# Sums over a head's 64 channels: one fp32 product, or two fp32r products on data split into high and low parts

## The chip, the cores and the metric

The kernel runs on one core of a Trainium2 chip. The metric is the device time of one execution in microseconds (us). Matrix products run on TensorE (PE in the profile), elementwise work on VectorE (DVE), ScalarE (ACT) and GpSimd (POOL), and transfers are started by SyncE (SP).

## The reference, cut to what matters

One layer of a streaming encoder is computed for 1024 prompt frames and 64 sample frames. Each frame is normed, projected to 3336 columns, and split between an RWKV-7 group (8 heads of 64 channels, with a recurrent state) and a forgetting-attention group (8 heads of 64 channels). The two are joined, projected, and followed by a SwiGLU feed-forward part. Five places need, for each head and frame, a sum or a mean over the head's 64 channels:

```
kk = kk / jnp.maximum(jnp.linalg.norm(kk, axis=-1, keepdims=True), 1e-12)
bonus = (jnp.sum(rh * kh * r_k, axis=-1, keepdims=True) * vh).reshape(b, t, RWKV_WIDTH)
mu = jnp.mean(y, axis=-1, keepdims=True)
var = jnp.mean(jnp.square(y - mu), axis=-1, keepdims=True)
q = _rms_norm(_heads(q, FOX_HEADS), fox_q_g)      # and the same for the keys
```

All of it is fp32.

## The kernel before, in words

**Layout.** Channels lie on the 128 partitions and frames along the free axis, so that one tile holds two heads (a pair is called j, 0 to 3). The frames are cut into two halves: half 0 has 512 frames, half 1 has 512 and the 64 sample frames, 576 in all. A half's `chunks` (L46) are the pieces that one product covers: one of 512 columns, or two of 288.

**Large products** are made from fp32r operands, each split into a high part (a rounding copy on ACT) and a low part (the difference, on DVE), as three products: high by high, high by low, low by high (`mm3`, L318). The projections write the PSUM tile `pmm` this way.

**Sums over a head** are made by `bsum` (L398): a product with a 128x128 matrix of ones in two 64x64 blocks (`bones`), or of 1/64 (`bmean`). Both matrices and the data are plain fp32, and there is one product for each chunk. The PSUM tile is `pbs`. There are 48 calls, 24 for each half: per head pair two in `rwkv_a` (on `sq` and on `zr`, which is a tile called `z` in the profile), two in `rwkv_n` (on `y` and on its squares, `gsq`), and two in `fox_norm` (on `fsq`, for queries and keys).

**The stages of an RWKV head pair.** `Z` makes three projections, `D` the decays, `A` (`rwkv_a`) the sums, the products `pA` and a small triangular inverse that goes through DRAM, `B` (`rwkv_b`) first completes the inverse with small products (`pg`, `pw`, `pu`, `pgt`) and then runs the scan: 8 or 9 steps, each of the products `pR`, `pSA`, `pS` and two `pY`, with copies on DVE and ACT between them, each step waiting for the one before it. `N` (`rwkv_n`) normalises `y`. The stages `Q`, `K` project attention's queries and keys and `q`, `k` norm them; `V` makes values, `L` the forget biases, `O` writes rows of ones. The two strings in L35 are the order in which the program writes these stages for the two halves. In half 0 it reads `... A0 D1 Z1 L Q0 B0 V0 N0 A1 ...`, so `A1` is written behind `N0`. In half 1 it has `A2 k0 D3 Q1 q0 N0 B1`.

**What sets the order of the work.** A scheduler takes the program's instructions and puts each engine's in an order of its own: what is ready goes first, and among what is ready what was written first. Tiles come from pools; a pool has a number of slots for each tag, and a tile that finds no free slot holds its first writer back. Among the tags are `ms` (one slot in the kernel before), `sa`, `fx` (4 slots: two pairs of `fraw` and `fsq`), `rk` and `kb` (2 slots each), and for PSUM `ra`, `rb`, `fx`, `ch`, `mm`. `bsum` in `A` writes to `ra`, in `N` to `rb`, in `q` and `k` to `fx`. What fills PE between the steps of a scan is mostly projections.

**Attention** follows: eight heads of half 0 (`attend`), whose products of queries and keys are `psc`, with a product that adds the causal mask (`cmask`, L943); `ppt` are transposes and `pav` the products with the values. `att_pools` (L863) makes the mask in a slot of `ms` (`cm`, L871 to 876). The last `N3` of half 1 is written after the order strings are through (L1478) and ahead of attention. Then attention of half 1, the output projection, and the feed-forward part follow, none of which uses `bsum`.

Of the kernel before, what the change touches and what calls it, by code (L numbers as in the profile page):

```python
# [7 lines left out]
F32 = mybir.dt.float32  # L8
F32R = mybir.dt.float32r
BF16 = mybir.dt.bfloat16  # L10
AF = mybir.ActivationFunctionType
ALU = mybir.AluOpType
# [4 lines left out]
P = 128  # L17
# [3 lines left out]
SS = 64  # L21
# [43 lines left out]
class K:  # L65
# [47 lines left out]
    def consts2(self):  # L113
        nc, A = self.nc, self.A
        c, f = self.cpool, self.fper
        self.bones = f.tile([P, P], F32, name="bones")
        self.bmean = f.tile([P, P], F32, name="bmean")
        for t, v in ((self.bones, 1.0), (self.bmean, 1.0 / 64)):
            nc.gpsimd.memset(t, 0.0)
            nc.gpsimd.memset(t[0:64, 0:64], v)  # L120
            nc.gpsimd.memset(t[64:128, 64:128], v)
        self.tri = f.tile([P, P], F32, name="tri")
        nc.gpsimd.memset(self.tri, 1.0)
        nc.gpsimd.affine_select(out=self.tri, in_=self.tri, compare_op=ALU.is_ge, fill=0.0, base=0,
# [271 lines left out]
            evac(ps[:, 0:n], off, n)  # L396

    def bsum(self, hf, w, x, evac, tag):  # L398
        nc = self.nc
        for off, n in hf.chunks:  # L400
            ps = self.ps([P, 512], tag=tag, name="pbs")
            nc.tensor.matmul(ps[:, 0:n], w, x[:, off:off + n], start=True, stop=True)  # L402
            evac(ps[:, 0:n], off, n)

    def split_lora(self, hf, z):
# [280 lines left out]
    def logf(self, hf):  # L686

        nc, O = self.nc, self.O
# [6 lines left out]
        for off, n in hf.chunks:  # L695
            ps = self.ps([P, 512], tag="mm", name="pfl")
# [8 lines left out]
        for i in range(nt):  # L705
            m = P if i < 4 else SS
# [4 lines left out]
        w = self.fpool.tile([P, 5, 8], F32, tag="lfw", name="lfw")  # L711
# [33 lines left out]
            nc.gpsimd.tensor_copy(keep, acc)  # L745
            self.lacc = keep

        q4 = self.fpool.tile([P, 7, 4, 8], F32, tag="lq", name="lq")
        hi = self.fpool.tile([P, 7, 2, 8], F32R, tag="lh", name="lh")
        for i, _, _, _, _ in order:  # L750
            nc.vector.tensor_copy(hi[:, i, 0], pl[:, i])
# [5 lines left out]
        for g in (order[0:4], order[4:]):  # L757
# [11 lines left out]
            w = sum(m for _, _, _, m, _ in g)  # L769
# [67 lines left out]
    def by_tokens(self, hf, j, src):  # L837
        nc = self.nc
        pt = self.ps([P, 4, P], tag="fx", name="pkv")
        for i in range(4):  # L840
            nc.tensor.transpose(pt[:, i], src[:, i * P:(i + 1) * P], self.ident)
        dst, ds_ = self.slot([P, 4, P], name="tok", tag="fx"), None
        nc.scalar.copy(dst, pt)
        nc.sync.dma_start(self.O["fox_v"][j, :, 4 * hf.i:4 * hf.i + 4], dst)
        if hf.smp:
            pt = self.ps([SS, P], tag="fx", name="pkvs")
            nc.tensor.transpose(pt, src[:, 512:576], self.ident)
            ds_ = self.fpool.tile([SS, P], F32, tag="toks", name="toks")
            nc.scalar.copy(ds_, pt)
            nc.sync.dma_start(self.O["fox_v"][j, 0:SS, 8], ds_)  # L850
        return dst, ds_
# [518 lines left out]
    def run(self):  # L1370
        tc, nc, A, O = self.tc, self.nc, self.A, self.O
        halves = [Half(0), Half(1)]
        with ExitStack() as top:
            E = lambda es, name, bufs=1, **k: es.enter_context(tc.tile_pool(name=name, bufs=bufs, **k))
# [20 lines left out]
            mid = top.enter_context(ExitStack())  # L1395
            self.cmid = E(mid, "cmid")
            self.consts()
            self.spool = MultiPool({"mrow": E(mid, "smrow", 2), "mred": E(mid, "smred", 2)})
            self.spool.pools.update({"ms": E(mid, "sms", 1)})
            hst = top.enter_context(ExitStack())  # L1400
            hp = E(hst, "hpool", side="right")
            self.hhi = hp.tile([P, KT, 576], F32R, name="hhi")
# [2 lines left out]
            with ExitStack() as es:  # L1405
# [3 lines left out]
                hf = halves[0]  # L1409
# [4 lines left out]
                raw, w = [], []  # L1414
# [26 lines left out]
            E = lambda es, name, bufs=1, **k: E0(es, name, bufs, **{"reuse_waits": "tile", **k})  # L1441
# [8 lines left out]
            FP = lambda p, tags: MultiPool({t: E(fxs, p + t, b, side="right") for t, b in tags})  # L1450
            RP = lambda p, tags: MultiPool({t: E(rws, p + t, b) for t, b in tags})
            self.rpool.pools.update(RP("r", (("pp", 1), ("pb", 2), ("mb", 1), ("wb", 1), ("tb", 1), ("xl", 1))).pools)
            self.spool.pools.update(RP("s", (("sa", 4),)).pools)
            self.fpool = FP("f", (("toks", 1), ("lfu", 1), ("lfe", 1), ("lfw", 1), ("lacc", 2), ("lq", 1), ("lh", 1)))
            self.spool.pools.update(FP("s", (("fx", 4),)).pools)
            self.ops = {}

# [11 lines left out]
            for hf in halves:  # L1469
                if hf.i:  # L1470
                    for k in range(KT):
                        x = self.zpool.tile([P, 576], F32, tag="z", name="xk")
# [81 lines left out]
            acc, raw, w, ada = None, [], {}, []  # L1554
# [208 lines left out]
```

## Time and profile before

| | |
|---|---|
| time, median of 3 runs | 1698.58 us (1694.36 to 1699.02) |
| profiled execution, span from first to last instruction | 1691.4 us |
| median less span | 7.2 us |
| PE busy | 1642.2 us, 97% |
| DVE busy | 1122.1 us, 66% |
| ACT busy | 725.6 us, 43% |
| mean granted PE clock | 0.992 |
| `bsum` products, first and last | 68.9 us, 722.6 us |

The profile is of one execution, and gives no time of its own beside the span; what lies around the span is taken as the 7.2 us between it and the median. [...] One fp32 product is two MATMUL rows in the trace and one row in the order.

### The profile page before, as it was taken

What the parts mean: (1) busy time and instruction counts of PE and PEld (TensorE: products, weight loads), DVE (VectorE), ACT (ScalarE), POOL (GpSimd) and SP (SyncE); (2) the same over time, 40 slices, a digit from 0 to 9 for tenths busy, and PEclk for the clock granted to TensorE, in tenths of its full rate; (3) what the DMA queues carried; (4) which work ended last, traced back from release to release, by engine and by line L of the source; (5) the groups of instructions that cost most, each with busy time, mean ns of one, the idle gap of its engine ahead of it and who ended that gap; (6) DMA issues with size and microseconds to landing.
All of it is one profiled execution on the core that took longest, in us unless ns stands there. A gap on an engine that the chain in (4) does not pass through costs nothing.

```text
span 1691.4 us, 33224 instructions
## 1 busy us (share of the span) xinstructions
PE 1642.2 (97%) x12891; PEld 1438.5 (85%) x12891; DVE 1122.1 (66%) x2561; ACT 725.6 (43%) x1524; POOL 184.7 (11%) x412
## 2 busy tenths in 40 slices
PE   6999999999999999989999999999999999999999
PEld 3776776788888888667889899999999999999998
DVE  6776676757867655886887985555555556545545
ACT  4535364653545345775776633333333333111210
POOL 2102230222121212201220000000000000000000
PEclk9999999999999999998999999999999999999999
DMA  8544447541233344466564532222222215423313
GB/s 310 163 129 132 141 136 201 175 124 33 72 85 85 81 136 115 144 203 177 156 194 153 178 121 78 77 77 77 78 77 77 77 65 178 146 87 97 97 38 125
DMA packets 133580, 207.08 MB, mean 122 GB/s; under 512 B 62126, under 2 KB 70350, under 8 KB 133422
## 3 DMA queue, kind: packets, MB, share of 16 engines
q1 hardware_dynamic: 133422, 204.95, 39.6%
q8 instruction: 102, 1.67, 0.4%
q14 instruction: 56, 0.46, 0.1%
HBM read 157.65 MB, written 47.25 MB: 121 GB/s over the span
## 4 chain that ended last, share of the span: by engine, by line
PE 85%; ACT 5%; DVE 5%; DMA 4%; issue 2%; SPq 0%; ACTq 0%; DVEq 0%
PE pd L1302 15%; PE pfe L1187 8%; PE pfc L1187 7%; PE pfa L1187 7%; PE pmm L321 5%; PE pmm L322 5%; PE pmm L323 5%; PE pfb L1187 4%; PE pbs L402 2%; PE pav L989 2%; PE ppt L967 2%; PE pA L491 2%; PE po L321 2%; PE po L322 2%; PE po L323 2%
## 5 line engine op out<-in xcount | busy, mean ns | idle before, releaser
L321 PE MATMUL pmm<-hhi,whi 128*128 128x288 f32 (+1 forms) x624 | 218.2, 350 | 2.4 <-ACT pb L344 1.4
L322 PE MATMUL pmm<-hlo,whi 128*128 128x288 f32 (+1 forms) x624 | 216.4, 347 | 0.7 <-DVE hlo L299 0.7
L323 PE MATMUL pmm<-hhi,wlo 128*128 128x288 f32 (+1 forms) x624 | 214.7, 344 | 0.6 <-DVE wlo L243 0.6
L239 ACT CAST whi<-wraw 128x1024 fp32r<-128x1024 f32 (+2 forms) x116 | 99.2, 855 | 210.0 <-PE pd L1302 163.6
L1302 PE MATMUL pd<-al,whi 128*128 128x512 f32 (+1 forms) x528 | 172.4, 326 | 0.0
L1302 PE MATMUL pd<-ah,whi 128*128 128x512 f32 (+1 forms) x528 | 172.2, 326 | 0.0
L1302 PE MATMUL pd<-ah,wlo 128*128 128x512 f32 (+1 forms) x528 | 172.2, 326 | 0.0
L1306 DVE SCALAR_TENSOR_TENSOR x1t<-pd,mod,x1t 128x512 f32<-128x512 f32 x192 | 91.2, 498 | 106.6 <-PE pd L1302 105.9
L321 PEld LDWEIGHTS pmm<-hhi,whi 128*128 128x128 f32 x624 | 118.4, 190 | 13.9 <-ACT pb L344 2.0
L322 PEld LDWEIGHTS pmm<-hlo,whi 128*128 128x128 f32 x624 | 118.2, 189 | 10.9 <-DVE hlo L299 1.4
L323 PEld LDWEIGHTS pmm<-hhi,wlo 128*128 128x128 f32 x624 | 118.1, 189 | 10.7 <-issue 1.7
L243 DVE TENSOR_TENSOR wlo<-wraw,whi 128x1024 fp32r<-128x1024 f32 (+2 forms) x108 | 104.2, 964 | 19.5 <-ACT whi L239 18.7
L1302 PEld LDWEIGHTS pd<-ah,whi 128*128 128x128 f32 x528 | 99.1, 188 | 7.1
L1302 PEld LDWEIGHTS pd<-ah,wlo 128*128 128x128 f32 x528 | 99.1, 188 | 7.1
L1302 PEld LDWEIGHTS pd<-al,whi 128*128 128x128 f32 x528 | 99.1, 188 | 6.9
L1187 PE MATMUL pfc<-hh,hS 128*128 128x256 f32 (+1 forms) x352 | 101.8, 289 | 1.1 <-ACT hh L1089 1.1
L1187 PE MATMUL pfa<-hh,whi 128*128 128x256 f32 (+1 forms) x352 | 102.1, 290 | 0.0
L1187 PE MATMUL pfc<-hh,lS 128*128 128x256 f32 (+1 forms) x352 | 101.8, 289 | 0.0
L1187 PE MATMUL pfa<-hl,whi 128*128 128x256 f32 (+1 forms) x352 | 101.6, 289 | 0.0
L1187 PE MATMUL pfa<-hh,wlo 128*128 128x256 f32 (+1 forms) x352 | 101.5, 289 | 0.0
L1187 PE MATMUL pfc<-hl,hS 128*128 128x256 f32 (+1 forms) x352 | 100.7, 286 | 0.0
L631 POOL TENSOR_SCALAR sd<-sv,pc 64x64 f32<-64x64 f32 x136 | 77.0, 566 | 181.3 <-DVE sv L644 157.7
(368 smaller groups left out, 4380.7 us busy)
## 6 DMA issues: line engine op xcount, KB each, us to landing
wraw<-in_w_in_dram SPq DMA_DIRECT2D x52, 512.0 KB
wada<-in_w_ada_dram SPq DMA_DIRECT2D x48, 512.0 KB
as<-actscr SPq DMA_DIRECT2D x22, 544.0 KB
wraw<-in_w_gate_dram SPq DMA_DIRECT2D x22, 512.0 KB
wraw<-in_w_up_dram SPq DMA_DIRECT2D x22, 512.0 KB
wraw<-in_w_down_dram SPq DMA_DIRECT2D x40, 256.0 KB
wraw<-in_w_out_dram SPq DMA_DIRECT2D x16, 512.0 KB
actscr<-sg SPq DMA_DIRECT2D x22, 288.0 KB
```

What stands on the lines that cost most here:

```text
L239: nc.scalar.copy(hi, src)
L243: eng.tensor_tensor(lo, src, hi.bitcast(F32), op=ALU.subtract)
L321: nc.tensor.matmul(ps[0:M, 0:n], whi[:, k, 0:M], xhi[:, k, off:off + n], start=(k == 0), stop=False)
L322: nc.tensor.matmul(ps[0:M, 0:n], whi[:, k, 0:M], xlo[:, k, off:off + n], start=False, stop=False)
L323: nc.tensor.matmul(ps[0:M, 0:n], wlo[:, k, 0:M], xhi[:, k, off:off + n], start=False, stop=(k == kt - 1))
L402: nc.tensor.matmul(ps[:, 0:n], w, x[:, off:off + n], start=True, stop=True)
L491: nc.tensor.matmul(pa[h][:, i], kb[hp, c + i], rk[hp, c + i], start=True, stop=True)
L631: nc.gpsimd.tensor_scalar(sd[hsl[h]], sv[hsl[h], c, h], pc[hsl[h], c], None, op0=ALU.mult)
L967: nc.tensor.transpose(pt[0:rows, b - b0, t * P:t * P + qn], p[0:qn, pc:pc + rows], self.ident[0:qn, 0:qn])
L1187: nc.tensor.matmul(ps, l[:, k], r[:, s, k], start=(first and k == 0 and y == 0), stop=(k == 3 and y == 2), skip_group_check=True)
L1302: nc.tensor.matmul(ps[:, 0:n], w[:, i], x[:, t:t + n], start=(i == 0 and y == 0), stop=(i == len(fs) - 1 and y == 2))
L1306: nc.vector.scalar_tensor_tensor(dst, ps[:, so - off:so - off + l], self.mod[:, 40 + o, b:b + 1], dst, op0=ALU.mult, op1=ALU.add)
```

## The change

`bsum` splits its data into a high part (copy to fp32r on ACT) and a low part (difference on DVE), both in a new tile `bhl`, and makes two fp32r products, ones by high and ones by low, that add up in PSUM. `bones` and `bmean` become fp32r. The pieces are 256 columns in half 0 and 288 in half 1, so half 0 has two for each call, and its PSUM tiles and evacuations are of 256 columns. `bhl` is a tile of `ms`, which gets three slots. To make room, two small tiles (`lq`, `toks`) move from pools of their own to slots of `ms` and `mrow`.

```diff
     def consts2(self):
-        self.bones = f.tile([P, P], F32, name="bones")
-        self.bmean = f.tile([P, P], F32, name="bmean")
...
+        self.bones = f.tile([P, P], F32R, name="bones")
+        self.bmean = f.tile([P, P], F32R, name="bmean")
+        blk = self.slot([P, P], name="blk")
...
+        nc.vector.tensor_copy(self.bones, blk)
+        nc.vector.tensor_scalar(self.bmean, blk, 1.0 / 64, None, op0=ALU.mult)
...
     def bsum(self, hf, w, x, evac, tag):
-        for off, n in hf.chunks:
+        m = 288 if hf.smp else 256
+        for off, n in ((o, m) for o in range(0, hf.n, m)):
+            hl = self.slot([P, 2, 288], F32R, name="bhl")[:, :, 0:n]
+            nc.scalar.copy(hl[:, 0], x[:, off:off + n])
+            nc.vector.tensor_tensor(hl[:, 1], x[:, off:off + n], hl[:, 0].bitcast(F32), op=ALU.subtract)
             ps = self.ps([P, 512], tag=tag, name="pbs")
-            nc.tensor.matmul(ps[:, 0:n], w, x[:, off:off + n], start=True, stop=True)
+            for i in range(2):
+                nc.tensor.matmul(ps[:, 0:n], w, hl[:, i], start=(i == 0), stop=(i == 1))
             evac(ps[:, 0:n], off, n)
...
-        q4 = self.fpool.tile([P, 7, 4, 8], F32, tag="lq", name="lq")
+        q4 = self.slot([P, 7, 4, 8], name="lq")
...
-            ds_ = self.fpool.tile([SS, P], F32, tag="toks", name="toks")
+            ds_ = self.slot([P, P], name="toks", tag="mrow")[0:SS]
...
-            self.spool.pools.update({"ms": E(mid, "sms", 1)})
+            self.spool.pools.update({"ms": E(mid, "sms", 3)})
```

The change also moves work on every engine. Throughout the changed kernel the casts into `bhl` stand in the order in which the program makes the tiles. Three places follow; a number behind a name tells tiles of one name apart, and line numbers of the changed kernel are larger by 8 behind `bsum`.

ACT, first half, before: `sq_1151` is the tile of `A1`, and L460 and L461 work on its sums. These rows stand 76 rows ahead of the first row of `N0` on this engine (the squares `gsq_1791`).

```order
L703 COPY fl_1263<-pfl_1267 128x512
L194 COPY mrow_1360<-pada_1351 128x128
L460 ACTIVATE sq_1151<-sq_1151 128x512
L718 ACTIVATE lfe_1291<-lfu_1290 128x32
L461 ACTIVATE sq_1151<-sq_1151 128x512
L719 ACTIVATE lfe_1291<-lfe_1291 128x32
```

ACT, first half, changed: `y_1585` and `gsq_1818` are tiles of `N0`, `sq_1167` is the tile of `A1`.

```order
L406 CAST bhl_1811<-y_1585 128x256
L241 CAST whi_2799<-wraw_2797 128x1024
L196 COPY mrow_2740<-pada_2731 128x128
L672 ACTIVATE gsq_1818<-y_1585 128x512
L406 CAST bhl_1820<-gsq_1818 128x256
L406 CAST bhl_1827<-gsq_1818 128x256
L406 CAST bhl_1843<-sq_1167 128x256
L674 ACTIVATE gsq_1818<-pbs_1823,eps_g_156 128x256
L406 CAST bhl_1850<-sq_1167 128x256
```

The sums of `A1` moved from well ahead of `N0` to behind both sums of `N0`, and with them what needs them: the `pA` products of `A1` and its inverse.

PE, half 1, the middle of the scan of pair 0, before: one step from its `pR` on, with projections (`pmm`) between its products.

```order
L624 MATMUL pR<-sv,At 128x128
L635 MATMUL pY<-rk,sv 128x128
L322 MATMUL pmm<-hlo,whi 128x288
L323 MATMUL pmm<-hhi,wlo 128x288
L321 MATMUL pmm<-hhi,whi 128x288
L637 MATMUL pSA<-R,inv_692 128x64
L322 MATMUL pmm<-hlo,whi 128x288
L323 MATMUL pmm<-hhi,wlo 128x288
L321 MATMUL pmm<-hhi,whi 128x288
L322 MATMUL pmm<-hlo,whi 128x288
```

PE, the same scan, changed: two of its last five steps, all of which look like this.

```order
L632 MATMUL pR<-sv,At 128x128
L643 MATMUL pY<-rk,sv 128x128
L645 MATMUL pSA<-R,inv_686 128x64
L648 MATMUL pS<-sv,kb 128x128
L653 MATMUL pY<-At,sv 128x128
L632 MATMUL pR<-sv,At 128x128
L643 MATMUL pY<-rk,sv 128x128
L645 MATMUL pSA<-R,inv_686 128x64
L648 MATMUL pS<-sv,kb 128x128
L653 MATMUL pY<-At,sv 128x128
```

No projection stands between their products any more. The scan of pair 2 of this half has six such steps at its end, and those of pair 2 in half 0 and pair 3 in half 1 have some too. After the small products that follow this scan, PE has 20 `bsum` products in a row.

PE, the end of half 1, before: attention's first rows, the mask among them. They stand ahead of the first `pR` of the last scan (pair 3).

```order
L937 MATMUL psc<-k1x_8027,qsx_8025 128x256
L939 MATMUL psc<-k2x_8028,q2x_8026 128x256
L943 LDWEIGHTS identb
L943 MATMUL psc<-cmask,identb 128x128
L550 MATMUL pu_8122<-inv_693,g_8059 32x32 x18
L841 MATMUL pkv<-ident,fv 128x128 x2
```

PE, the end of half 1, changed: the last step of the last scan, and the first rows with the mask.

```order
L632 MATMUL pR<-sv,At 128x128
L645 MATMUL pSA<-R,inv_687 128x64
L643 MATMUL pY<-rk,sv 128x128
L648 MATMUL pS<-sv,kb 128x128
L653 MATMUL pY<-At,sv 128x128
L410 MATMUL pbs<-bhl,bmean 128x288 x6
L951 LDWEIGHTS identb
L951 MATMUL psc<-cmask,identb 128x128
```

The mask, and with it all of attention but four `psc` products, moved from ahead of the last scan to behind it and behind six of the eight products of `N3`. On POOL the instruction that fills `cm` moved from an early place in half 0 to behind the last scan's rows (`sd`).

## The prediction on record

> **What bounds the kernel now.** I read first the page's busy line, which names PE.
>
> ```profile
> PE 1642.2 (97%) x12891; PEld 1438.5 (85%) x12891; DVE 1122.1 (66%) x2561; ACT 725.6 (43%) x1524; POOL 184.7 (11%) x412
> ```
>
> A busy share over the whole span can hide a stage with another limit, so the timeline was next, for marks. A scan begins with a `pR`; these are the first `pR` of the first scan, the second, the fourth, the fifth and the last, with the first product of the last `N` behind them.
>
> ```profile
> 148.76 0.46 PE L624 MATMUL pR<-sv,At 128*128 128x128 f32 x2
> 211.50 0.46 PE L624 MATMUL pR<-sv,At 128*128 128x128 f32 x2
> 378.30 0.46 PE L624 MATMUL pR<-sv,At 128*128 128x128 f32 x2
> 468.73 0.46 PE L624 MATMUL pR<-sv,At 128*128 128x128 f32 x2
> 678.36 0.46 PE L624 MATMUL pR<-sv,At 128*128 128x128 f32 x2
> 717.43 0.70 PE L402 MATMUL pbs<-y,bmean 128*128 128x288 f32 x2
> ```
>
> Between these marks the windows view gives PE alone: the stretch, its length, PE's busy time, the granted clock.
>
> ```profile
> 0.00:148.80 148.80, 131.32 (x1142) 0.98 0.58 194
> 148.80:211.50 62.70, 61.35 (x544) 1.00 0.46 131
> 211.50:378.30 166.80, 161.75 (x1408) 0.99 0.55 161
> 378.30:468.70 90.40, 88.40 (x830) 1.00 0.20 49
> 468.70:678.40 209.70, 204.99 (x1947) 0.99 0.39 103
> 678.40:717.40 39.00, 35.19 (x229) 1.00 0.50 149
> 717.40:945.00 227.60, 218.71 (x1330) 0.97 0.60 175
> ```
>
> In every stretch but the first, where loads come in, PE is busy for 90% or more. Two things run side by side: a chain (sums, inverse, scan, norm, pair after pair), which is a matter of waits, and projections, which fill PE while the chain waits. So PE's work sets the time only as long as there is something to fill with. The rest of the span, behind 945 us, has no `bsum`, and I leave it as it is.
>
> **What the change takes from PE.** These rows give the distance between ends: a 512-column fp32 product behind the product before it, a 288-column one likewise, and neighbours of 256 and 288 columns among the fp32r products of the feed-forward part.
>
> ```profile
> 68.53 0.50 PE L321 MATMUL pmm<-hhi,whi 128*128 128x512 f32 x1
> 68.87 1.02 PE L402 MATMUL pbs<-sq,bones 128*128 128x512 f32 x2
> 551.73 0.29 PE L323 MATMUL pmm<-hhi,wlo 128*128 128x288 f32 x1
> 551.86 0.65 PE L402 MATMUL pbs<-sq,bones 128*128 128x288 f32 x2
> 1100.77 0.29 PE L1187 MATMUL pfb<-hl,hS 128*128 128x288 f32 x1
> 1100.90 0.30 PE L1187 MATMUL pfb<-hh,lS 128*128 128x288 f32 x1
> 1110.15 0.28 PE L1187 MATMUL pfa<-hh,whi 128*128 128x256 f32 x1
> 1110.27 0.28 PE L1187 MATMUL pfa<-hl,whi 128*128 128x256 f32 x1
> ```
>
> The view of L402 counts the fp32 products by shape, two MATMULs each; the `z`, `y` and `gsq` groups have the counts of `sq`.
>
> ```profile
> L402 PE MATMUL pbs<-fsq,bones x48: 404/432/697, 154.5 to 653.8; 128*128 128x288 f32 x32, 128*128 128x512 f32 x16
> L402 PE MATMUL pbs<-sq,bones x24: 403/406/697, 68.9 to 552.1; 128*128 128x288 f32 x16, 128*128 128x512 f32 x8
> ```
>
> 512 columns: 69.89 less 69.03 is 0.86 us. 288 columns: 552.51 less 552.02 is 0.49. The new ones: 0.12 for 256, 0.13 for 288. A call in half 0 goes from 0.86 to 4 x 0.12 = 0.48, and 24 of them save 9.1 us. A piece in half 1 goes from 0.49 to 0.26, and 48 save 11.0. In all 20 us leave PE, 1.2% of the time. If PE's work were all, that would be the result.
>
> **What it adds.** 96 casts and 96 subtracts. The nearest rows are those of attention's `pth` and `ptl`, of 256 columns.
>
> ```profile
> 718.50 0.37 ACT L980 CAST pth<-ppt 128x256 fp32r<-128x256 f32 x1 [0.49 <-PE ppt L967]
> 720.58 0.40 DVE L981 TENSOR_TENSOR ptl<-ppt,pth 128x256 fp32r<-128x256 f32 x1
> ```
>
> 96 x 0.37 is 36 us on ACT and 96 x 0.40 is 38 us on DVE, spread over some 650 us in which neither bounds: hidden as work, and paid only as delay, 0.8 us ahead of each sum. Without that cover, both engines' 74 us would be the bound on it, and nothing in the profile puts them in line.
>
> **What it moves.** This decides. `bhl` has three slots for all 48 calls, and the slots go in program order. Before, the sums of `A`, `N` and `q`/`k` waited only for PSUM slots of their own (`ra`, `rb`, `fx`); now a sum that is not ready holds up every later one. `A1` is written behind `N0`, so its sums wait for the whole first scan; the order of ACT shows that. The rows of the chain before: the first sum of `A0`, the end of its `pA`, its first `pg`; the first sum of `A1`; the last product of the first scan; the first sum of `N0`.
>
> ```profile
> 88.80 0.94 PE L491 MATMUL pA<-rk,kb 64*128 64x128 f32 x7
> 132.96 0.24 PE L550 MATMUL pg<-gt,At 32*32 32x32 f32 x2
> 100.28 1.13 PE L402 MATMUL pbs<-sq,bones 128*128 128x512 f32 x2
> 182.55 0.39 PE L645 MATMUL pY<-At,sv 128*128 128x128 f32 x2
> 184.78 1.02 PE L402 MATMUL pbs<-y,bmean 128*128 128x512 f32 x2
> ```
>
> *Up to the first scan.* What moved out of this stretch is worth about 16 us of PE, counted in the order: 34 projection products, half of the `pA`, 17 rows of the conditioning, and the smaller sums. PE was full, so it shrinks from 149 to 132 (-17).
>
> *First scan to second.* The scan keeps its 34 us (148.8 to 182.9). Then come the sums of `N0`, which began 2 us behind the scan's last product, and their casts and subtracts: I count 6 us until the first sum of `A1`. From there `A0` took 20.8 us to the end of `pA` (68.9 to 89.7), 43.3 to `pg` (132.96) and 15.8 to `pR` (148.76): 80 us, with PE and DVE full of other work between its links. What the order gives PE in this gap is some 46 us of work. So the gap is between 46 and 80, and I take 64, since part of `A0`'s 80 was waiting its turn. 34 + 6 + 64 = 104 instead of 62.7 (+41; ends +17 and +57).
>
> *Second to fourth.* The scan of pair 2 runs out of projections and the sums of `N2` come alone behind it, about 6 us of casts, subtracts and evacuations that PE only waits for; less work in the stretch before it gives 4 back: +2 (ends -10 and +12).
>
> *Fourth to fifth.* The first `A` of half 1 has its `pA` behind that scan, where it stood inside it. `pA` to `pR` was 59 us above, so 8 + 59 = 67 less the 53 that stood between these scans: +14, or less where waiting shrinks. I take +10 (ends 0 and +18).
>
> *Fifth to last.* Two scans have five and six steps without a projection. A step's length is its chain, though, and not PE's work:
>
> ```profile
> 633.79 0.46 PE L624 MATMUL pR<-sv,At 128*128 128x128 f32 x2
> 638.14 0.38 PE L624 MATMUL pR<-sv,At 128*128 128x128 f32 x2
> ```
>
> 4.35 us a step with 16 projections of 0.13 us in it. A bare step will not be shorter by more than a few tenths, and the fill it lost is done elsewhere, some of it where PE would wait. 20 sums in a row, with casts and evacuations of a piece about 1 us in line, stand where the norm stood before. +4 (ends -6 and +12).
>
> *The last scan and attention.* The mask's `cm` is a fourth kind of tile in `ms` and is written behind `N3`, so attention starts when the last scan is over. Before, it began at 666.8:
>
> ```profile
> L943 PE MATMUL psc<-cmask,identb x72: 213/231/330, 666.8 to 882.9; 128*128 128x128 bf16 x64, 64*64 64x64 bf16 x8
> ```
>
> In the windows view of `pav`, `ppt` and `psc` alone (first column behind the length: PE's busy time, and the count) this is what ran beside the last scan.
>
> ```profile
> 678.40:717.40 39.00, 10.26 (x48) 6.99 (x48) 1.00 0.50 149
> 678.40:717.40 39.00, 7.67 (x40) 4.74 (x40) 1.00 0.50 149
> 678.40:717.40 39.00, 6.43 (x16) 2.94 (x16) 1.00 0.50 149
> ```
>
> 48 `pav` of 256 columns at 0.12 us are 5.8 us, about half of their busy time, since rows overlap. Half of the other two gives 3.8 and 3.2, and the second product of `psc` and the mask about 4 more: 17 us of PE that now lie behind the scan, on the path. Attention's own start (first product, maximum, exponential, transposes) is no longer covered, 8 us: +25 (ends +10 and +35).
>
> The constants, `lq`, `toks` and the rows of ones each take a slot for a few us, beside other work: nothing.
>
> Sum: -17 + 41 + 2 + 10 + 4 + 25 = +65. The 20 us that PE saves are in these stretches already. On the span that is 1756.4 us, with the 7.2 us around it 1763.6: **1764 us**.
>
> [...] Where PE had gaps, the profile shows a lower granted clock:
>
> ```profile
> 726.00:740.00 14.00, 10.63 (x61) 8.46 (x61) 11.72 (x34) 8.67 (x27) 1.28 (x8) 0.88 0.67 205
> ```
>
> but 678.4 to 717.4, with 35.2 of 39 us busy, was granted 1.00. Bare steps have PE busy for barely a third. [...] The sum above goes by full clock; the other way is the second rival.
>
> **The rivals.**
>
> *PE's work decides* (it ends on the other side): the scheduler fills every gap, and PE stays 97% busy. Then 1698.6 - 20 = 1678 us. For it: the windows above. Against it: bare steps in four scans, which leave nothing to fill with. It decides if the first gap is no longer than its 46 us of work and attention's start is hidden.
>
> *Half clock in the bare stretches*: some 18 bare steps each hold five fp32 products of 128 columns or fewer, by the 512-column row about 0.86 x 128 / 512 = 0.22 us. At half rate a step gets 1.1 us longer, 18 of them 20 us, on top of the forecast: 1784 us. It decides if the clock in those scans is granted below 0.7.
>
> *Losses and gains cancel*: the gap behind `N0` at its lower end (+17), attention's start at +10, the others at 0 and the first stretch at -17: +10, and with the stretch from second to fourth at its lower end 0: 1699 us.
>
> *The sums cost what they did*, if two fp32r products with ones ran at fp32 speed: +20 on the forecast. The feed-forward rows speak against it; I give it no chance of its own.
>
> **How the numbers follow.** Forecast 0.70, half clock 0.13, PE's work 0.12, cancelling 0.05. The first two are slower: 0.83. Adding all lower ends gives -6 and all upper ones +122; they won't fall together, so the forecast's own range is about +10 to +106, 1708 to 1805, which holds the second rival too. Taking 1705 to 1805 leaves out PE's work and most of cancelling, 0.17. A measurement of this kernel tells about 0.3% (5 us) from no change: its runs lie 4.7 us apart.
>
> **What would show it.** Right: the first `pR` near 132 us and the second scan near 236; PE's busy share well down between them; `cmask` products only behind the last scan; starved scans of the old length; `bsum` at 0.12 to 0.13 us between ends. Wrong: the second scan starting before 215 us, or attention beginning beside the last scan, or a span under 1700 us.

## The result, and the profile after

The changed kernel takes 1866.44 us (median of 4 runs, 1864.31 to 1869.41), the kernel before 1696.86 (4 runs): ratio 1.1007, 95% interval 1.0994 to 1.102, or 170 us more. The forecast was 1764 us, with a range to 1805. The direction was right; 105 us of loss were not in the sum. Of the page after, PE's busy line comes first, and the row of the granted clock in 40 slices.

```profile
PE 1712.6 (92%) x12939; PEld 1502.3 (81%) x12939; DVE 1163.6 (62%) x2671; ACT 760.6 (41%) x1632; POOL 183.1 (10%) x409
PEclk9999669969997899587899999999999999999999
```

The same row before:

```profile
PEclk9999999999999999998999999999999999999999
```

PE has less work to do, 20 us by the prediction's count, and is busy 70 us longer (1712.6 against 1642.2), over slices in which its granted clock was lower. The marks after, from the timeline: the first `pR` of the first scan, the second, the fourth, the fifth and the last, and the first product of the last `N`.

```profile
135.66 0.49 PE L632 MATMUL pR<-sv,At 128*128 128x128 f32 x2
266.52 0.77 PE L632 MATMUL pR<-sv,At 128*128 128x128 f32 x2 [0.92 <-ACT sv L613]
453.84 0.49 PE L632 MATMUL pR<-sv,At 128*128 128x128 f32 x2
558.63 0.46 PE L632 MATMUL pR<-sv,At 128*128 128x128 f32 x2
805.30 0.46 PE L632 MATMUL pR<-sv,At 128*128 128x128 f32 x2
845.41 0.85 PE L410 MATMUL pbs<-bhl,bmean 128*128 128x288 f32 x2 [0.56 <-DVE y L658]
```

Between them, in the windows view: the stretch, its length, the busy time of PE, its weight loads, DVE, ACT and POOL, then the granted clock.

```profile
0.00:135.70 135.70, 112.61 (x1040) 79.67 (x1040) 86.10 (x226) 61.71 (x121) 20.79 (x73) 0.97 0.59 198
135.70:266.50 130.80, 96.60 (x712) 72.55 (x712) 77.50 (x211) 48.98 (x109) 14.46 (x35) 0.79 0.29 83
266.50:453.80 187.30, 167.73 (x1330) 131.95 (x1330) 116.34 (x294) 94.63 (x214) 39.26 (x69) 0.85 0.48 134
453.80:558.60 104.80, 97.62 (x901) 87.22 (x897) 78.65 (x235) 48.77 (x114) 18.01 (x43) 0.95 0.20 53
558.60:805.30 246.70, 215.42 (x1841) 183.44 (x1842) 136.90 (x378) 102.44 (x264) 45.37 (x91) 0.81 0.29 76
805.30:845.40 40.10, 30.73 (x157) 24.85 (x157) 17.82 (x54) 16.04 (x46) 12.86 (x20) 0.76 0.32 94
845.40:1100.00 254.60, 234.71 (x1372) 189.89 (x1373) 191.02 (x428) 169.19 (x395) 32.36 (x78) 0.94 0.58 165
```

Before, these stretches were granted 0.97 to 1.00. A granted clock of 0.50 stands in both traces: after, from 828.04 to 836.70 us in the last scan, and before for 2 us behind the last scan, with PE busy throughout:

```profile
730.00:732.00 2.00, 2.00 (x10) 1.93 (x10) 1.69 (x6) 1.75 (x5) 0.41 (x2) 0.50 0.78 227
```

If all the clock that is missing is read as time at this half rate, a stretch of length L at clock k holds 2 x (1 - k) x L of it: 55 us between the first and second scan, 56 to the fourth, 10 to the fifth, 94 to the last, 19 in the last, 31 behind it. Over the whole profile (span 1863.4 us, mean clock 0.927) it is 272 us, before (1691.4 at 0.992) 27.

The wait that the prediction spoke of is there too. In the gap behind the first scan, in order: `N0`'s first sum, the first product of `A1`'s first sum, its `pA`, its first `pg`.

```profile
167.56 0.42 PE L410 MATMUL pbs<-bhl,bmean 128*128 128x256 f32 x2
172.37 0.28 PE L410 MATMUL pbs<-bhl,bones 128*128 128x256 f32 x1
187.66 2.40 PE L499 MATMUL pA<-rk,kb 64*128 64x128 f32 x16 [0.20 <-DVE bon L488]
248.08 0.24 PE L558 MATMUL pg<-gt,At 32*32 32x32 f32 x2
```

The first products of the mask, 184 us later than before, and behind the last scan:

```profile
L951 PE MATMUL psc<-cmask,identb x72: 213/231/331, 850.5 to 1052.8; 128*128 128x128 bf16 x64, 64*64 64x64 bf16 x8
```

### The profile page after: what moved, and what is told of

The parts are those of the page before. It is cut to its first block, busy times and chain, and to the rows that moved or that the text cites. A ratio compares the mean times of both kernels' runs of the same rounds, so it can differ in the third digit from the quotient of the medians.

```text
span 1863.4 us, 33588 instructions
## 1 busy us (share of the span) xinstructions
PE 1712.6 (92%) x12939; PEld 1502.3 (81%) x12939; DVE 1163.6 (62%) x2671; ACT 760.6 (41%) x1632; POOL 183.1 (10%) x409
## 4 chain that ended last, share of the span: by engine, by line
PE 78%; DVE 8%; ACT 7%; DMA 3%; issue 3%; SPq 1%; DVEq 0%; ACTq 0%; POOL 0%
PE pd L1310 14%; PE pfe L1195 7%; PE pfc L1195 7%; PE pfa L1195 7%; PE pmm L323 5%; PE pmm L324 5%; PE pmm L325 5%; PE pfb L1195 3%; PE pbs L410 2%; PE pav L997 2%; PE pA L499 2%; PE ppt L975 2%; PE pS L648 1%; PE po L324 1%; PE po L323 1%
## 5 line engine op out<-in xcount | busy, mean ns | idle before, releaser
L323 PE MATMUL pmm<-hhi,whi 128*128 128x288 f32 (+1 forms) x624 | 222.0, 356 | 11.7 <-ACT fsq L794 4.3
L323 PEld LDWEIGHTS pmm<-hhi,whi 128*128 128x128 f32 x624 | 124.0, 199 | 24.5 <-ACT fsq L794 5.5
L325 PEld LDWEIGHTS pmm<-hhi,wlo 128*128 128x128 f32 x624 | 122.9, 197 | 9.4 <-DVE wlo L245 0.9
L324 PEld LDWEIGHTS pmm<-hlo,whi 128*128 128x128 f32 x624 | 123.5, 198 | 8.2 <-issue 0.5
```

The lines of the kernel that those rows point to most:

```text
L323: nc.tensor.matmul(ps[0:M, 0:n], whi[:, k, 0:M], xhi[:, k, off:off + n], start=(k == 0), stop=False)
L324: nc.tensor.matmul(ps[0:M, 0:n], whi[:, k, 0:M], xlo[:, k, off:off + n], start=False, stop=False)
L325: nc.tensor.matmul(ps[0:M, 0:n], wlo[:, k, 0:M], xhi[:, k, off:off + n], start=False, stop=(k == kt - 1))
```

## The experiments

Two theories stood at the start. *Slots*: sums that have nothing to do with each other wait for each other in the order of the slots of `ms`, and that is the loss. *Steps*: the cast and the subtract ahead of every sum are the loss. *Clock* joined them as a third. All times are medians of 4 runs or more, and the ratio is to the kernel before on the same chip (its median lay between 1694 and 1697 us).

### Slots: taken apart, and made without a split

*Own slots.* `bhl` of `A`, of `N` and of `q`/`k` each get one slot of their own; `ms` goes back to one slot, and small tiles move to make room.

```diff
-            hl = self.slot([P, 2, 288], F32R, name="bhl")[:, :, 0:n]
+            hl = self.slot([P, 2, 288], F32R, name="bhl", tag={"ra": "ha", "rb": "hn", "fx": "hq"}[tag])[:, :, 0:n]
```

> The changed kernel with three tags of one slot each for the split data, one for the sums of A, one for those of N, one for those of q and k, in place of three slots that all share; ms has one slot again (the forget biases' small tile, the rows of ones and the raw weights of the small projections move to other tags to make room). Theory 1 (the sums wait for each other in program order): the time falls from 1866 to 1676 to 1700 us, no scan step on PE is bare, the granted clock is back at 0.98 or more, and the second scan begins before 220 us. Theory 2 (the split itself, a cast and a subtract ahead of each sum, is what costs): it stays over 1780 us. Theory 3 (half clock alone costs, whatever sets it off) gives no number of its own here, but wants clock and time to move together.

Measured: 1790.25 us, ratio 1.0566 (1.0522 to 1.0611). Against the changed kernel's 170 us, 74 come back and 96 stay. That is a time that the second theory named (over 1780), and not the 1676 to 1700 of the first, so undoing the sharing, with one slot for each kind in place of three for all, gives back less than half of the loss. The 74 hold the mask's part too, since its first product comes at 757.5 us here, ahead of the last scan (777.9). The first two stretches of this kernel:

```profile
0.00:142.20 142.20, 113.78 (x1017) 80.52 (x1018) 85.73 (x224) 60.84 (x122) 22.07 (x74) 0.94 0.52 175
142.20:256.90 114.70, 90.66 (x698) 68.23 (x697) 75.63 (x213) 48.56 (x109) 17.40 (x34) 0.85 0.36 103
```

The second scan is still late, though `A1`'s sums wait no longer for `N0`. The trace has the four products of `A1`'s first sum spread from 113.6 to 139.7 us: each has its cast or subtract ahead of it, and two pieces share one slot. Which of these drew them out was not separated here.

*Coupled without a split.* A plain fp32 copy of each operand goes through three slots of `ms`, and the plain product follows; `lq` and `toks` are moved as in the change, the constants are as before.

```diff
+            cp = self.slot([P, 576], name="bcp")[:, 0:n]
+            nc.scalar.copy(cp, x[:, off:off + n])
...
-            nc.tensor.matmul(ps[:, 0:n], w, x[:, off:off + n], start=True, stop=True)
+            nc.tensor.matmul(ps[:, 0:n], w, cp, start=True, stop=True)
```

> The kernel before with its plain fp32 product, but each piece of data first copied in fp32 on ACT to a slot of ms, which has the three slots of the changed kernel, with lq and toks moved as there. So it has the shared slots and a copy, and neither the split nor the fp32r products. Theory 1: over 1800 us, with bare steps and a mean clock under 0.96. Theory 2: at most 1720 us, since one copy of 0.4 to 0.6 us is all that is added.

Measured: 1851.0 us, ratio 1.0915 (1.0896 to 1.0935). No fp32r product, no subtract, and 157 us of loss. Not all of it is due to the slots: by the runs below, the moves cost 36 us alone and two steps ahead of each sum 34. If these simply add, 87 us or more are left for the shared slots. The second stretch is close to that of the kernel after, and its clock too:

```profile
137.70:266.80 129.10, 99.91 (x719) 69.87 (x719) 72.29 (x193) 46.96 (x99) 14.40 (x35) 0.82 0.31 90
```

*The mask in a slot of another tag* (`cm` to `mrow`), and *`A1` written ahead of `B0`* (`"B0 V0 N0 A1 C0"` becomes `"A1 B0 V0 N0 C0"`), each on the kernel after:

> The changed kernel with only the mask's cm moved to a slot of another tag (mrow), so that attention need not wait for the last N. Theory 1: attention's first mask product comes ahead of the end of the last scan, and 30 to 45 us go: 1820 to 1836 us. My prediction's term for this was 25 us. If attention's late start costs nothing: 1861 us or more.

> The changed kernel with A1 written ahead of B0, V0 and N0 in the first half's order string, nothing else. Theory 1: the gap between first and second scan falls from 103 us to 40 to 60, and the time by 40 to 65 us: 1800 to 1825 us. Theory 2: no change beyond 10 us.

Measured: 1853.92 us (ratio 1.0937, 1.0909 to 1.0965) and 1839.77 us (1.0849, 1.0804 to 1.0894). Neither time lies where a theory put it. The first gave back some 10 us (170 less 160), but it moved the mask only in part: `mrow` also holds `toks`, and the mask was filled at 822.7 us, inside the last scan, with its first product at 824.9 (850.5 after, 666.8 before). So 10 us is not the whole price of the mask's late place, and no run measured that price alone. With `A1` ahead, the second scan begins at 199.9 us, 29 us behind the last `pR` of the first (103 after), but the sums and `pA` of the next pair now stand inside its first step, which lasts 13.4 us. The third scan follows 129 us behind the second's start (84 before, 88 after): the wait went on to the next pair, and only 24 us came back.

### Steps, and one kind of sum at a time

*The two steps in place*, in the kernel before, with no slot and the plain product:

```diff
+            xs = x[:, off:off + n]
+            nc.scalar.copy(xs, xs)
+            nc.vector.tensor_tensor(xs, xs, xs, op=ALU.max)
```

> The kernel before, with the two steps that the split puts ahead of each product (one on ScalarE, one on VectorE, on the same pieces of 256 or 288 columns), but both in place on the operand and with the plain product: no extra slot, so no sum can wait for another's slot. Theory 'slots' (the sums wait for each other through the shared slots): the two steps alone cost little, 1695 to 1725. Theory 'steps' (the two steps' own time on the way to each product, and on their engines, make up the 96 us that stay when each consumer has its own slot): 1765 to 1800. Theory 'clock' (PE's half clock sets in by itself when its work is split): mean clock stays at 0.98 or above here, as the products are the old ones; if it falls below 0.96 with these, the waits make the clock and not the products.

*One kind split*, the others plain, all else as after (`if tag != ...` ahead of the split):

> The kernel after with only the sums over q and k split; those in A and N are the plain fp32 product again (one for each chunk). Theory 'slots': a sum waits for one of another kind, so one kind alone costs little, 1690 to 1720. Theory 'steps': q and k lie off the chain of the scans, 1695 to 1715; the three kinds alone then add up to +96 us or more. Under 'slots' the three alone add up to under 60 us.

> The kernel after with only the two sums of A split (three slots for them alone); N, q and k plain. Theory 'slots': 1690 to 1720. Theory 'steps': A stands on the way to each scan, 1745 to 1790.

> The kernel after with only the two sums of N split; A, q and k plain. Theory 'slots': 1690 to 1720, with the mask's slot still behind the last N's sums (the attention some 10 us late). Theory 'steps': N follows its scan and nothing of the next scan waits for it, 1695 to 1715.

Measured: 1728.96 us in place (ratio 1.0206, 1.0186 to 1.0226); q and k alone 1742.84 (1.0277, 1.026 to 1.0294), `A` alone 1747.91 (1.0321, 1.0299 to 1.0343), `N` alone 1774.55 (1.0464, 1.0445 to 1.0483). "Slots" missed all four, the first by 4 us; "steps" had only `A` alone (1745 to 1790). The steps in place cost 34 us, a third of what they should, and one kind alone costs 48, 53 and 80, where no other kind's sums are in its slots. But all three one-kind kernels share the start that the expectation of the next run describes, so something that is no split was at work.

### The moves

*No split at all, the rest of the change kept*:

> The kernel after with no sum split at all (the plain fp32 product for all three kinds, one for each chunk); what stays of the change are its moves: three larger ms slots, the fox gate's lq in ms, the values' toks in mrow, the ones in fp32r read as fp32. The three kernels with one kind split began scan 0 at about 135 us and scan 1 at 220 to 226, whichever kind it was, and in the order this kernel has A1's pA inside scan 0 too, where the kernel before has it ahead. Theory 'moves' (the slots' moves alone reorder the start, and each one-kind kernel paid for them): 1735 to 1755, scan 1 near 225. Theory 'kinds' (each kind's split costs 48 to 80 us by itself): 1690 to 1705.

(Its three slots are of the old size, as no `bhl` is in them.) Measured: 1732.23 us, ratio 1.0228 (1.0191 to 1.0266), a loss of 36 us with no sum split, close to "moves" and far from "kinds". Its second and third stretch, in the slowest of its four executions (1744.17 us):

```profile
133.00:226.00 93.00, 79.59 (x597) 56.18 (x598) 56.10 (x161) 31.52 (x72) 13.54 (x30) 0.81 0.30 83
226.00:327.70 101.70, 99.67 (x766) 72.11 (x764) 67.22 (x164) 50.20 (x101) 15.36 (x33) 0.99 0.61 178
```

The first scan starts 16 us earlier, the third 32 us later. Then which move? With one slot in `ms` again, and with `lq` and `toks` back in their pools as well:

> The kernel with the change's moves and no split (1732 us), with one slot in ms again in place of three: what stays are lq in ms, toks in mrow and the constants in fp32r. In its order A1's pA stands among the first products of pair 0's inverse, not inside scan 0. Theory 'three slots' (the looser slots let the start fall into another order, and that order costs the 39 us): 1693 to 1710. Theory 'lq' (the fox gate's lq waits in ms behind other tiles): 1725 to 1740.

> As that one, with lq and toks back in their own pools: only the constants differ from the kernel before (made through one ms tile, kept in fp32r and read as fp32). Its order of the start is that of before. Both theories: 1692 to 1702.

Measured: 1740.15 us (ratio 1.0268, 1.0246 to 1.0291) and 1701.24 us (1.0032, 1.0017 to 1.0046). So it is the move of `lq` and `toks`, 39 us, and not the number of slots; the constants take 6. The stretches of the first of the two:

```profile
141.30:221.70 80.40, 66.47 (x525) 44.16 (x526) 51.20 (x153) 29.58 (x68) 14.17 (x30) 0.81 0.31 84
221.70:321.40 99.70, 96.66 (x747) 68.80 (x747) 63.36 (x158) 49.02 (x100) 15.54 (x33) 0.95 0.59 177
```

In both kernels with these moves `A1`'s `pA` runs from 118.8 to 130.7 us (torn apart by the first inverse) or from 134.8 to 141.4 (inside the first scan), where it ended at 125 us before. `lq` itself holds nobody up for more than 2 us in the trace, so it is the order of the start that changed. Why the order answers to these tiles, and which of the two does it, wasn't tried.

*One kind split with nothing else moved*: the kernel before, with one slot added for that kind.

> The kernel before with only the sums over q and k split, in one slot of their own that is added behind the others (nothing else moved). Theory 'moves': 1688 to 1705. Theory 'kinds': about 1735 to 1745 as with q and k alone in the three shared slots.

> The kernel before with only N's two sums split, in one slot of their own; lq, toks, ms and the mask's slot as before. Theory 'moves': 1688 to 1710. Theory 'kinds': 1740 or above (without the 30 us that the mask's slot added to the attention's start when N's sums went through ms).

> The kernel before with only A's two sums split, in one slot of their own; nothing else moved. A's sums lie on the way to each scan. Theory 'moves': 1700 to 1725 (eight times 1 to 4 us for the two steps and the one slot). Theory 'kinds': 1745 or above.

Measured: 1724.43 us (ratio 1.0167, 1.0122 to 1.0213), 1739.27 (1.0252, 1.023 to 1.0274) and 1732.83 (1.0219, 1.0187 to 1.0252). Less than with the moves (by 18, 35 and 15 us), but 28, 43 and 37 us are lost where "moves" allowed at most 9, 14 and 29 and "kinds" asked for 39, 44 and 49 or more: neither had them. Each of these has its mean clock down, at 0.978, 0.972 and 0.969. That led back to the clock.

### The clock

Over the first twelve kernels and the two given ones the span follows the time at half clock nearly in a line, 0.7 us for each us of it (correlation 0.99). That may be cause or mark. To tell, the kernel after got extra products, read by nobody, in 22 scan steps that had little else on PE: 12 ahead of `pSA` and 12 ahead of `pS`, over 128 columns or over 2.

```diff
+            warm = c in {(0, 2): (4, 5, 6, 7), (1, 0): (4, 5, 6, 7, 8), (1, 2): (2, 3, 4, 5, 6, 7, 8), (1, 3): (3, 4, 5, 6, 7, 8)}.get((hf.i, j), ())
+            for _ in range(12 if warm else 0):
+                nc.tensor.matmul(pS.rearrange("p h t -> p (h t)")[:, 0:128], self.bones, self.bones[:, 0:128], start=True, stop=True)
```

> The kernel after, with products that nothing reads (12 of 128x128 in fp32r between pR and pSA and 12 more ahead of pS's own product, into pS, which that product then overwrites) in 22 scan steps that have little or no other work on PE: scan 2 from its 5th step, scan 4 from its 5th, scan 6 from its 3rd, scan 7 from its 4th. Over the 12 profiles with their kernels the span grows with the time at the half clock (from 28 us before to 274 after). Theory 'clock' (the half clock that sets in in these steps lengthens what follows): clock above 0.95, the half clock time down by 100 us or more, 1790 to 1835. Theory 'effect' (the half clock only marks places where PE waits anyway): the clock rises, the time stays, 1855 or above.

> As with the 12 and 12 products, but each over 2 columns in place of 128: the same instructions in nearly the same order, with little work in them. Theory 'clock': it stays cold, 1855 to 1875, as after. If this kernel gains as much as the other, the products' place in the order did it and not the clock.

Measured: 1880.93 us wide (ratio 1.1095, 1.1071 to 1.1119), 1946.19 thin (1.1478, 1.1457 to 1.1499). The wide kernel lies where "effect" put it (1855 or above), the thin one 71 us above anything expected: 24 products were too many for the waits of a step. Windows over three scans of the wide kernel:

```profile
558.60:600.00 41.40, 38.73 (x383) 34.95 (x383) 23.34 (x80) 20.91 (x53) 13.51 (x25) 1.00 0.26 66
742.00:786.00 44.00, 41.27 (x412) 38.04 (x410) 18.94 (x72) 9.58 (x35) 8.13 (x18) 1.00 0.33 85
820.00:866.00 46.00, 39.70 (x298) 36.79 (x298) 19.69 (x56) 16.06 (x45) 13.23 (x20) 0.96 0.29 85
```

and of the thin one:

```profile
575.00:637.00 62.00, 55.73 (x336) 51.14 (x337) 23.47 (x74) 12.52 (x39) 13.18 (x27) 0.68 0.15 35
761.00:830.00 69.00, 62.21 (x306) 57.33 (x304) 16.89 (x65) 9.48 (x34) 8.88 (x18) 0.60 0.20 51
868.00:930.00 62.00, 55.19 (x300) 50.80 (x299) 17.32 (x52) 16.42 (x45) 12.88 (x20) 0.68 0.21 61
```

The same number of products, in nearly the same order, and the kernel with 64 times fewer columns in them is 65 us slower. With a mean clock of 0.945 and 0.909 the two hold 207 and 354 us of half clock. But half of the 65 us is the added products' own time: both groups of twelve together keep PE busy for 104.4 us thin and 72.1 wide. In the thin kernel's trace twelve in a row take 1.34 us at full clock (593.88 to 595.22) and 2.56 at half (600.09 to 602.65), and of the 66 us between the two traces 51 lie inside the eight scans, where these products run. So the pair shows a row of products that took 1.9 times as long at half clock, and gives no price for a kernel without them. With 4 and 4 products:

> The kernel after with 4 and 4 products of 128x128 in the 22 scan steps in place of 12 and 12 (which held the clock in those scans at 0.96 to 1.00, but took 0.137 us each, 3.3 us a step). 1.1 us a step fits beside the waits of a step. Theory 'clock': the clock holds nearly as well, the steps are no longer than after's, 1815 to 1850. Theory 'effect': 1860 to 1875.

> Its thin twin, 4 and 4 products over 2 columns. The wide and the thin kernel with 12 and 12 were 65 us apart (1880.9 and 1946.2), with 210 and 356 us at half clock. Theory 'clock': again slower than its wide twin, by 20 us or more. Theory 'effect': within 5 us of it or faster.

Measured: 1866.48 us wide (ratio 1.1008, 1.0974 to 1.1042) and 1876.29 thin (1.1058, 1.1028 to 1.1088), at clocks of 0.932 and 0.924. Eight products didn't hold the clock (254 us at half, against 272 after), so the wide one didn't gain, as "effect" had it. Its twin is 9.8 us slower, which is neither the 20 of "clock" nor the 5 of "effect"; the eight scans of the twin are 15 us longer together, of which the added products' own time is 1 us (busy for 37.2 us thin, 36.2 wide).

A price without added products can be estimated from the executions of one kernel, which has the same instructions in the same order on PE each time. With one slot for `q` and `k` alone, the runs of 1716.56 and 1732.47 us had clocks of 0.981 and 0.968, or 65 and 111 us of half clock: 0.35 us lost for each. With `A1` ahead, 1829.85 and 1846.42 us came with 0.935 and 0.925, 238 and 277 us: 0.42. A line through the four runs of each of the four kernels whose runs lie over 30 us of half clock apart has a slope of 0.37 to 0.41. By that estimate the 245 us of half clock that the change added are some 90 to 100 of the 170 us. It stays an estimate: a wait that is longer in one execution could lower the clock and lengthen the time by itself, and no kernel held the clock without a cost of its own.

## Why the prediction was wrong, point by point

**The first stretch** was right: the first `pR` at 135.7, forecast 132.

**Slots as the mechanism** was right. `A1`'s sums do wait for `N0`, coupling without a split costs 157 us (with the moves and a copy in it), and undoing the sharing gives 74 back.

**"First scan to second" (+41, ends +17 and +57)** failed in its size: +68. Up to `A1`'s first sum it held (36.7 us, forecast 40). The term that failed is the gap behind it: "I take 64, since part of `A0`'s 80 was waiting its turn". It measured 94 (172.4 to 266.5), more than `A0`'s 80: 21 us to the end of `pA` (`A0` 20.8), 55 from there to `pg` (43.3) and 18 to `pR` (15.8). In the middle link PE also made the sums and `pA` of the next pair, at a granted clock of 0.74 (187 to 250 us). The stretch as a whole was granted 0.79; its 55 us of half clock are an estimated 20 to 23 of the 27 us missed.

**"Second to fourth" (+2), "fourth to fifth" (+10), "fifth to last" (+4)** became +20.5, +14.4 and +37. The scans themselves nearly kept their length, as forecast (from first to last `pR`, the first 30.2 us before and 28.0 after, the last 34.1 and 35.2, all eight 254 and 263); the gaps between them grew. Bare steps were put at "not shorter by more than a few tenths" than 4.35 us. In the last scan after, a step without projections at full clock is followed by one in which the clock falls and by bare ones at half:

```profile
820.60 0.46 PE L632 MATMUL pR<-sv,At 128*128 128x128 f32 x2 [0.43 <-DVE sv L652]
824.28 0.46 PE L632 MATMUL pR<-sv,At 128*128 128x128 f32 x2 [0.56 <-DVE sv L652]
828.04 0.77 PE L632 MATMUL pR<-sv,At 128*128 128x128 f32 x2 [0.35 <-DVE sv L652]
832.37 0.77 PE L632 MATMUL pR<-sv,At 128*128 128x128 f32 x2 [0.35 <-DVE sv L652]
```

3.68 us at a granted clock of 1.00, 3.76 at 0.78, then 4.33 from 828.04 on at 0.50: a step without projections is shorter by 0.7 us, and the clock takes that back. "Bare steps have PE busy for barely a third" was off as well: PE is busy for 3.11 of those 4.33 us.

**The last scan and attention (+25)**: the mask came behind the last scan as forecast. What follows the last `N`'s first product grew by 44 us, and the last scan by 1: 20 more than forecast. The mask's experiment gave 10 us back, with attention still starting inside the last scan, so this term was not measured by itself.

**"The sum above goes by full clock; the other way is the second rival"** is, as far as is known, the step that failed most: it put at nothing what the runs show as 245 us more of half clock, by the estimate above 90 to 100 us of time. The second rival, whose half rate the trace before shows, as in the 2 us above (0.50), named what came, with the wrong reach: it counted the products of 18 bare steps at 1.1 us each, 20 us. In the last scan after, a step loses 0.65 us (3.68 to 4.33), and some ten steps are that slow, which is 7; the three scans that have them were granted 0.73, 0.67 and 0.77, so its condition (below 0.7) came true in one. The rest of the half clock lies in the gaps behind the scans, over sums, inverse and projections. Stretch by stretch the shortfall goes with it: from first to second scan 27 us missed and 55 us of half clock, to the fourth 18 and 56, to the fifth 4 and 10, to the last 33 and 94, over the last scan and behind it 20 and 50. That the two go together doesn't show how much of each shortfall is the clock's and how much is the waits' beside it; that stays open.

**"The constants, `lq`, `toks` and the rows of ones ... nothing"** failed as well. The two small tiles cost 39 us by themselves, in an order in which `A1` falls behind, and with it 60 to 70 us of half clock come (mean clock 0.972, against 0.989 without). In the kernel after this lies inside the stretches above and doesn't add to them. That the new order is what costs was argued from the traces and not tested.

**The casts** were right as work, with medians of 0.41 to 0.42 us on ACT. As delay the prediction gave them no term of their own, only 0.8 us ahead of each sum: in place, with no slot, the two steps cost 34 us.

How the loss falls into parts, by the runs: the moves alone cost 36 us, own slots 96, shared slots 170. The 60 us between the first two are steps and single slots only if the moves cost the same in both, which no run shows, since own slots move some small tiles elsewhere. None of the parts is free of the clock: its mean is 0.970 with the moves, 0.951 with own slots and 0.927 in the kernel after, against 0.992 before.

**The upper ends** of the stretches add up to +117, where the prediction says +122; its range doesn't hang on that.

**PE's 20 us** can't be seen in the time, though the new products did take 0.12 us between ends where they stood side by side at full clock (the rows at 172.25 and 172.37 us, which overlap with 0.28 us each; granted 1.00 from 172 to 173). No variant with a split came below the kernel before.

## What to carry to other kernels

Before a shared slot is given to a new tile, list which stages it puts into one order, and price that as a chain and not as work. Where a kernel keeps PE fed by filling one chain's waits with other work, price a thinner stretch at the half clock too (0.50 in bare steps here, 4.33 us against 3.68), for the stretch and for what follows it. Moving small tiles cost 2% here: build the change without its point first, and time that. When products are added to hold the clock, count their own time before reading the difference as the clock's.

## What the hardware showed that was not expected

**Half clock in steps with short waits.** The prediction's sum went by full clock in bare steps. In the last scan of the kernel after, whose rows stand above, the granted clock went from 1.00 (820.60 to 824.28 us) to 0.50 (from 828.04 on), and no wait of PE between the scan's start and there was longer than 1.23 us. In the kernel with only `N` split, the last scan had no projections and was granted 0.50 from its start to its end; the windows view and, from the timeline, one of its steps:

```profile
717.00:752.50 35.50, 25.90 (x83) 19.52 (x83) 8.43 (x33) 5.52 (x23) 7.04 (x16) 0.50 0.05 19
```

```profile
726.36 0.76 PE L638 MATMUL pR<-sv,At 128*128 128x128 f32 x2 [0.36 <-DVE sv L658]
726.92 0.63 PE L649 MATMUL pY<-rk,sv 128*128 128x128 f32 x2
727.74 0.69 PE L651 MATMUL pSA<-R,inv 128*128 128x64 f32 x2 [0.19 <-ACT R L641]
729.11 0.80 PE L654 MATMUL pS<-sv,kb 128*128 128x128 f32 x2 [0.69 <-ACT sv L653]
729.70 0.63 PE L659 MATMUL pY<-At,sv 128*128 128x128 f32 x2
730.69 0.76 PE L638 MATMUL pR<-sv,At 128*128 128x128 f32 x2 [0.36 <-DVE sv L658]
```

The longest wait of the step is 0.69 us, and PE is busy for 25.9 of the scan's 35.5 us.

**Busy PE at both clocks.** In the thin kernel PE was 90% busy at a granted clock of 0.60 (62.21 of 69 us), in the wide one, with the same number of added products in a step, 94% busy at 1.00 (41.27 of 44 us). The groups of the first twelve in each step, in the thin kernel, busy time and mean ns of one:

```profile
L643 PE MATMUL pS<-bones 128*128 128x2 f32 x264 | 52.1, 324 | 0.0
```

and in the wide one:

```profile
L643 PE MATMUL pS<-bones 128*128 128x128 f32 x264 | 35.8, 288 | 1.0 <-DVE state L657 1.0
```

52.1 us over 264 are 0.197 us for 2 columns, in scans granted 0.60 to 0.68; 35.8 are 0.136 for 128 columns, in scans granted 0.96 to 1.00. At full clock they took nearly the same: twelve in a row 1.34 us thin, 0.112 each, and 1.37 wide (594.34 to 595.71 us), 0.114 each. The two kernels differ in nothing but the columns of these products. With 4 and 4 of them the clocks were 0.924 thin and 0.932 wide.

**Projections at two speeds.** In the wide kernel, projections of 288 columns, inside the window from 820 to 866 us that was granted 0.96 as a whole:

```profile
832.96 0.44 PE L325 MATMUL pmm<-hhi,wlo 128*128 128x288 f32 x1
833.20 0.44 PE L323 MATMUL pmm<-hhi,whi 128*128 128x288 f32 x1
833.44 0.35 PE L324 MATMUL pmm<-hlo,whi 128*128 128x288 f32 x1
833.63 0.30 PE L325 MATMUL pmm<-hhi,wlo 128*128 128x288 f32 x1
833.76 0.29 PE L323 MATMUL pmm<-hhi,whi 128*128 128x288 f32 x1
833.89 0.33 PE L648 MATMUL pSA<-R,inv 128*128 128x64 f32 x2
```

0.24 us from start to start in the first rows, 0.13 in the last. That the clock rises between them is the author's reading of these distances.
